# Strided attention on one core: full-width products on TensorE, a 32-bit turn of the weights, and one store with another wait

## The chip, the cores and the metric

The kernel runs on one core of a Trainium2 chip. The metric is the device time of one execution in microseconds (us). Before the change three runs took 128.56, 128.7 and 128.8 us; their median is 128.7 us. One further execution was recorded by the hardware profiler, and all rows of the profile come from it.

The core has five engines that run side by side and wait for each other by semaphores: TensorE (PE in the profile; PEld is its loading of weights), VectorE (DVE), ScalarE (ACT), GpSimd (POOL) and SyncE (SP). SP only issues transfers here. All transfers go through one queue.

## The reference, cut to what matters

```python
batch, heads, seq, dim = (8, 12, 1024, 64)     # stride = 64
for i in range(seq):
    attend_positions = np.arange(0, seq, stride)            # 16 keys for every query
    scores = np.einsum('bhqd,bhkd->bhqk', q, k) * scale     # scale = 1 / sqrt(dim)
    weights = np.exp(scores - np.max(scores, axis=-1, keepdims=True))
    weights = weights / (np.sum(weights, axis=-1, keepdims=True) + 1e-10)
    result[:, :, i, :] = np.einsum('bhqk,bhkd->bhqd', weights, v)[:, :, 0, :]
```

Every query of a head sees the same 16 keys (positions 0, 64, 128, ...). Q is read whole and the result is written whole, 25 MB each; of K and V only 16 rows a head are read.

## The kernel before, in words

**Groups.** The 96 heads are worked on in 24 groups of four heads. A group of Q is 1 MB: 128 partitions with 32 queries of 64 numbers each, so a partition holds 32 x 64 float32 values. A buffer of `big` (16 of them, `NB`) receives a group of Q and later takes the group's result, which is stored from there.

**The stages of a group g**, with the engine and the line that carries each in the profile:

1. SP loads Q into `big` (L34).
2. ACT casts one half of it to 16 bits into `qb` (L352), POOL the other half (L357).
3. DVE turns `qb` into `qt` (L361), with a transpose that works on blocks of 32 x 32 words; a word is a pair of 16-bit numbers (even and odd dimension of Q).
4. PE multiplies keys and `qt`, giving the scores in the PSUM bank `sc` (L557). A group has two pairs of heads (index b) and two halves of the queries (index e). For each half f of the dimension, each e and each b there is one product with 32 columns of weights, `k_cur`, which lands on its own 32 partitions of the bank: 8 products with 512 columns of `qt`.
5. DVE turns the scores into `s_t` (L392), so that a partition again holds its 32 queries with 16 scores each, and finds the maximum of each query (`top`, L399).
6. POOL subtracts it (`diff`, L406), ACT takes the exponential (`ex`, L412), DVE adds up (`total`, L417) and inverts (`rec`, L424), POOL multiplies (`w_n`, 16 bits, L431).
7. DVE turns the weights back (`w_t`, L437), as 128 x 512 numbers of 16 bits, in one instruction.
8. PE multiplies `w_t` and the values `v_cur` (L571): for each half h of the result four steps, each with two products of 64 x 64 weights, one on the partitions and outputs 0 to 63, one on 64 to 127: 16 products a group.
9. ACT evicts each half from PSUM into `big` (`evict`, L453), and SP stores it (L34).

**Keys and values.** All keys and values are loaded, cast and arranged at the start (lines 297 to 346). After that POOL copies the keys of the next two groups into `k_cur` (`place_k`) and the values of two groups into `v_cur` (`place_v`), both through the helper of L370.

**What sets the order.** The program is written out by hand in the loop of lines 503 to 546: step n deals with the scores of group n, the turn of Q of group n + 1, the sums of group n - 1, the turned weights and outputs of group n - 2, and so on. Each engine works through its own part of that list in order. VectorE's order in a round is: `s_t` of g, `qt` of g + 1, `top` of g, `total` of g - 1, `w_t` of g - 2, `rec` of g - 1. For groups 2 to 21 these rounds are a hardware loop (`dve_stream`); PE runs a loop over all groups (`pe_stream`), with the scores of group j + 3 ahead of the outputs of group j. So at the end it still computes scores for the groups 24 to 26, which do not exist; nobody reads them.

**Waits.** An instruction may count up a named "gate" (`ev` for evictions, `wt` for turned weights, `wn`, `ex`, `sc`, `turned`, `stK`, `stV`), or the general semaphore of its engine, not both. Whoever wants to wait for a gated instruction in the general way waits for the next ungated one of that engine instead (lines 103 to 110):

```python
while d is not None and self.ops[d]["gate"]:
    later = (j for j in range(d + 1, i) if self.ops[j]["lane"] == p["lane"])
    d = next(later, None)
```

The stores wait for evictions in this way. Before the change all evictions except those of the last group carry the gate `ev` (L454). So the store of the groups 20 and 21, which needs the eviction (21, 1), waits for the next ungated instruction of ACT after it, the eviction (23, 0). The last store, of the groups 22 and 23, is issued by itself after everything else (L631).

Of the kernel before, what the change touches and what calls it, by code (L numbers as in the profile page):

```python
# [174 lines left out]
def kernel(  # L175
# [8 lines left out]
    nc = tc.nc  # L184

    B, H, S, D = Q.shape
    NK = S // stride
# [27 lines left out]
    diff = [sb.tile([P, 32, NK], FP32, name=f"diff{i}") for i in range(2)]  # L215
# [58 lines left out]
    def constants():  # L274
        op("POOL", lambda: nc.gpsimd.memset(identity, 0.0), writes=["identity"])
        op("POOL", lambda: nc.gpsimd.affine_select(
            out=identity, in_=identity, compare_op=ALU.not_equal, fill=1.0, base=0,
            pattern=[[-1, P]], channel_multiplier=1,
        ), reads=["identity"], writes=["identity"])
        for c in range(2):  # L280
            for b in range(2):
                op("POOL", lambda c=c, b=b: nc.gpsimd.tensor_copy(
                    out=perm_v[:, c, b],
                    in_=_ap_with(
                        identity, [identity.ap[0], [0, 2], [32, 2], [1, NK]], 64 * c + 16 * b
                    ),
                ), reads=["identity"], writes=[f"perm{c}{b}"])
        op("DVE", lambda: nc.vector.memset(k_all, 0.0), writes=["k_zero"])
# [78 lines left out]
    def place(to, from_, g, n, needs, writes, gate):  # L367
        dims = "pgabx"[: len(to.shape)]
        flat = f"{' '.join(dims)} -> p ({' '.join(dims[1:])})"
        op("POOL", lambda: nc.gpsimd.tensor_copy(  # L370
            out=to[:, g % 2 : g % 2 + n].rearrange(flat).bitcast(I32),
            in_=from_[:, g : g + n].rearrange(flat).bitcast(I32),
        ), reads=needs, writes=writes, gate=None if g == 1 else gate)

    def place_k(g):
        n = 1 if g < 2 else 2
        place(k_cur, k_all, g, n,
              ["k_zero"] + [f"k{i % 2}{s}" for i in range(g, g + n) for s in range(4)],
              [f"k_cur{i % 2}" for i in range(g, g + n)], "stK")

    def place_v(g):
        n = 1 if g < 2 else 2
        place(v_cur, v_all, g, n,
              [f"v_all{i % 2}{x}" for i in range(g, g + n) for x in range(4)],
              [f"v_cur{i % 2}" for i in range(g, g + n)], "stV")

    def scores(g):
        op("PE", None, reads=[f"qt{g % 2}", f"k_cur{g % 2}"], writes=[f"sc{g % 2}"],
# [15 lines left out]

    def subtract(g):
        op("POOL", lambda: nc.gpsimd.tensor_tensor(  # L406
            out=diff[g % 2], in0=s_t[g % 2],
            in1=top[g % 2].unsqueeze(2).to_broadcast([P, 32, NK]), op=ALU.subtract,
        ), reads=[f"s_t{g % 2}", f"top{g % 2}"], writes=[f"diff{g % 2}"])

    def raise_(g):
        op("ACT", lambda: nc.scalar.activation(  # L412
            out=ex[g % 2][:, :, 0:NK], in_=diff[g % 2], func=AF.Exp, bias=0.0, scale=scale,
        ), reads=[f"diff{g % 2}"], writes=[f"ex{g % 2}"], gate="ex" if g < LAST - 1 else None)

    def sums(g):
        return nc.vector.tensor_reduce(out=total[g % 2], in_=ex[g % 2], op=ALU.add, axis=mybir.AxisListType.X)  # L417
# [11 lines left out]

    def normalise(g):  # L430
        op("POOL", lambda: nc.gpsimd.tensor_tensor(  # L431
            out=w_n[g % 2], in0=ex[g % 2][:, :, 0:NK],
            in1=rec[g % 2].unsqueeze(2).to_broadcast([P, 32, NK]), op=ALU.mult,
        ), reads=[f"ex{g % 2}", f"rec{g % 2}"], writes=[f"w_n{g % 2}"], gate="wn")

    def back(g):
        return nc.vector.transpose(  # L437
            _ap_with(w_t[g % 2], [w_t[g % 2].ap[0], [64, 8], [1, 2], [2, 32]]),
            w_n[g % 2].rearrange("p n k -> p (n k)"),
        )  # L440
# [9 lines left out]
    def evict(g, h):  # L450
        o = o_ps[h].rearrange("p c (t x d) -> p x (c t) d", t=2, d=D)
        to = big[:, g % NB].rearrange("p (x t d) -> p x t d", x=4, t=8)[:, :, 4 * h : 4 * h + 4]
        op("ACT", lambda: nc.scalar.copy(to, o), reads=[f"o{h}"], writes=[f"b{g % NB}{'ab'[h]}"],  # L453
           gate=None if g == NG - 1 else "ev")  # L454

    first_loads()
    constants()
# [35 lines left out]
    def on(f, g, *a, **how):  # L493
        if 0 <= g < NG:
            f(g, *a, **how)
# [7 lines left out]
    for n in range(NG + 4):  # L503
        how = dict(looped=FIRST <= n < LAST, late=n >= LAST)
        on(evict, n - 3, 1)
        if n < NG:
            spread(n, **how)
        if n == 0:
            maximum(n)
        on(turn_over, n + 1, **how)  # L510
        if n == 0:
            value_blocks(0, range(2, 4))
        elif n < NG:
            maximum(n, **how)
        on(add_up, n - 1, **how)
        on(weights_back, n - 2, **how)
        on(invert, n - 1, **how)
        if n == NG - 1:
            for g in range(AHEAD):
                op("DVE", lambda: nc.vector.nop(), gate="turned", late=True)  # L520
        if n % 2 and n > 1:
            next_keys(n + 1)
        on(cast_p, n + 2)
        if n % 2 == 0 and n > 2:
            on(place_v, n - 2)
        if n < NG:
            subtract(n)
        if n == 1:
            next_keys(n + 1)
        if n == 1 or n == 2:  # L530
            place_v(n - 1)
        on(normalise, n - 1)
        if n + 1 < NG + AHEAD:
            scores(n + 1)
        for h in range(2):
            on(outputs, n - 2, h)
        on(cast_a, n + 3)
        if n < NG:
            raise_(n)
        if n < 2:  # L540
            value_blocks(1, range(2 * n, 2 * n + 2))
        if n == 1:
            load(NB - 2)
            load(NB - 1)
        on(evict, n - 2, 0)
        issue(n - 3 if n + 3 < NG else n - 4)
    issue(NG, flush=True)

    def pe_stream(sems, gates):
        pe = nc.tensor  # L550

        def score_products(g):
            for f in range(2):
                for e in range(2):
                    for b in range(2):
                        c = 2 * b + e
                        r = pe.matmul(  # L557
                            sc_ps[g % 2][32 * c : 32 * c + 32], lhsT=k_cur[:, g % 2, f, b],
                            rhs=_ap_with(
                                qt[g % 2], [qt[g % 2].ap[0], [D, 8], [16 * D, 2], [2, 32]],  # L560
                                extra_offset=8 * D * e + f,
                            ),
                            start=f == 0, stop=f == 1, tile_position=(0, 32 * c),
                        )
            r.then_inc(gates["sc"], 1)

        def output_products(g, h):
            for t in range(4):
                for b in range(2):
                    half_b = slice(64 * b, 64 * b + 64)  # L570
                    r = pe.matmul(  # L571
                        o_ps[h][half_b, t // 2, 256 * (t % 2) : 256 * (t % 2) + 256],
                        lhsT=w_t[g % 2][half_b, 4 * h + t],
                        rhs=v_cur[half_b, g % 2].rearrange("p x d -> p (x d)"),
                        start=True, stop=True, tile_position=(64 * b, 64 * b),
                    )
            r.then_inc(sems["PE"], 1)

        pe.wait_ge(gates["stV"], 1)
# [86 lines left out]
```

## Time and profile before

| | |
|---|---|
| median of three runs | 128.7 us (128.56 to 128.8) |
| the profiled execution | 128.46 us, of which the profile's span is 126.6 us |
| busy: PE, DVE, ACT, POOL | 64.2, 100.5, 90.2, 84.2 us |
| moved | 51.15 MB, 404 GB/s over the span |
| read from and written to HBM | 25.95 and 25.17 MB |

The rows read as follows. A group's row gives line, engine, operation, the tile written and the tiles read, the shape, the count, then the busy time and the mean duration in ns of one, then the idle time of the engine ahead of them and what ended it. A timeline row gives start and length, then the instruction; "x8" means that eight were merged into one row. A row of a stretch (from:to) gives its length, busy time and count for PE, PEld, DVE, ACT and POOL, then the clock granted to TensorE as a share of full speed, the transfers' busy share, and GB/s. Durations can be longer than the distance to the next instruction, because an engine may begin the next one while the last one's end is still under way; the chain of waits shows the distance, a group's mean the duration.

### The profile page before, as it was taken

The page shows a single profiled execution, that of the slowest core. Times are in us where ns is not written, and L with a number is a line of the kernel's source. Part 1 is how long each engine was busy: PE and PEld are TensorE (multiplying, and loading weights), DVE is VectorE, ACT ScalarE, POOL GpSimd, SP SyncE. Part 2 cuts the span into 40 slices and gives each one's busy share as a digit, 9 for nine tenths or more (in the row PEclk, how much of TensorE's full clock was granted, in tenths as well). Part 3 has the DMA queues.
Part 4 walks back from the last instruction along what each step waited for, and adds up shares of the span by engine and source line. Part 5 has one row for each costly group of instructions (what it writes and reads, how often), then busy time and mean ns, then how long its engine had stood idle before and what let it go on. Part 6 is the DMA issues. An engine that isn't in the chain of part 4 may idle for free.

```text
span 126.6 us, 1871 instructions
## 1 busy us (share of the span) xinstructions
PE 64.2 (51%) x604; PEld 32.7 (26%) x604; DVE 100.5 (79%) x159; ACT 90.2 (71%) x106; POOL 84.2 (67%) x110
## 2 busy tenths in 40 slices
PE   0000702338777788777345777779755336970000
PEld 0000100004543245543112543335522213530000
DVE  4329699499999999999999999999999999520000
ACT  4016679557899988989999789998899669692000
POOL 4016742859888898888898888898888867600000
PEclk9999999999999999999999555555589998699555
DMA  3899999999999989999999989989899999988993
GB/s 93 311 405 441 404 466 445 393 445 404 476 435 393 445 362 422 479 399 396 479 386 430 500 352 453 479 349 494 378 430 430 425 430 425 425 347 342 414 414 166
DMA packets 6803, 51.15 MB, mean 404 GB/s; under 512 B 3760, under 2 KB 3760, under 8 KB 3760
## 3 DMA queue, kind: packets, MB, share of 16 engines
q1 hardware_dynamic: 6800, 51.12, 96.5%
q14 instruction: 3, 0.02, 0.1%
HBM read 25.95 MB, written 25.17 MB: 404 GB/s over the span
## 4 chain that ended last, share of the span: by engine, by line
DVE 68%; ACT 6%; DMA 5%; PE 5%; issue 3%; POOL 3%; DVEq 1%; SPq 0%
DVE qt L361 20%; DVE s_t L392 12%; DVE top L399 11%; DVE total L417 11%; DVE w_t L437 9%; DMA big<-in_K_dram 5%; DVE rec L424 3%; ACT big L453 3%; PE sc L557 2%; PE o L571 2%; DVE v_all L339 2%; POOL qb L357 1%; POOL diff L406 1%; ACT k_all L308 1%; ACT qb L352 1%
## 5 line engine op out<-in xcount | busy, mean ns | idle before, releaser
L453 ACT COPY big<-o 128x1024 f32<-128x1024 f32 x48 | 46.2, 1016 | 8.4 <-PE o L571 8.4
L571 PE MATMUL o<-v_cur,w_t 64*64 64x256 bf16 x384 | 38.5, 361 | 21.1 <-DVE w_t L437 18.6
L571 PEld LDWEIGHTS o<-v_cur,w_t 64*64 64x64 bf16 x384 | 28.7, 142 | 40.5 <-ACT big L453 27.2
L557 PE MATMUL sc<-qt,k_cur 128*32 128x512 bf16 x216 | 25.2, 557 | 15.4 <-DVE qt L361 10.0
L431 POOL TENSOR_TENSOR w_n<-ex,rec 128x512 bf16<-128x512 f32 x24 | 25.4, 1057 | 8.9 <-DVE rec L424 8.9
L406 POOL TENSOR_TENSOR diff<-s_t,top 128x512 f32<-128x512 f32 x24 | 25.4, 1058 | 7.9 <-DVE top L399 7.9
L361 DVE STREAM_TRANSPOSE qt<-qb 128x1024 int32<-128x1024 int32 x24 | 28.8, 1202 | 0.0
L352 ACT CAST qb<-big 128x1024 bf16<-128x1024 f32 x24 | 25.2, 1054 | 0.0
L357 POOL CAST qb<-big 128x1024 bf16<-128x1024 f32 x24 | 25.0, 1043 | 0.0
L412 ACT ACTIVATE ex<-diff 128x512 f32<-128x512 f32 x24 | 15.3, 638 | 6.2 <-POOL diff L406 6.1
L437 DVE STREAM_TRANSPOSE w_t<-w_n 128x512 bf16<-128x512 bf16 x24 | 17.9, 746 | 1.6 <-POOL w_n L431 1.5
L392 DVE STREAM_TRANSPOSE s_t<-sc 128x512 f32<-128x512 f32 x24 | 16.1, 671 | 1.6 <-PE sc L557 1.6
L417 DVE TENSOR_REDUCE total<-ex 128x32 f32<-128x544 f32 x24 | 17.0, 707 | 0.3 <-ACT ex L412 0.3
L399 DVE TENSOR_REDUCE top<-s_t 128x32 f32<-128x512 f32 x24 | 15.5, 647 | 0.1
L557 PEld LDWEIGHTS sc<-qt,k_cur 128*32 128x32 bf16 x216 | 3.6, 103 | 26.9 <-DVE qt L361 19.8
L315 PE MATMUL o<-big,perm_v 128*128 128x384 bf16 x4 | 1.5, 520 | 12.8 <-POOL big L323 12.8
L424 DVE RECIPROCAL rec<-total 128x32 f32<-128x32 f32 x24 | 7.4, 308 | 0.0
L370 POOL COPY v_cur<-v_all 128x256 int32<-128x256 int32 (+1 forms) x13 | 5.0, 384 | 1.1 <-PE o L571 1.1
L370 POOL COPY k_cur<-k_all 128x128 int32<-128x128 int32 (+1 forms) x13 | 3.7, 281 | 2.1 <-ACT k_all L308 1.8
L298 ACT CAST big<-big 128x384 bf16<-128x384 f32 x1 | 0.5, 511 | 5.6 <-DMA big<-in_K_dram 5.6
L299 POOL CAST big<-big 128x384 bf16<-128x384 f32 x1 | 0.5, 507 | 5.6 <-DMA big<-in_K_dram 5.6
L301 DVE STREAM_TRANSPOSE big<-big 128x384 int32<-128x384 int32 x1 | 0.6, 579 | 4.3 <-POOL big L299 4.3
(18 smaller groups left out, 18.8 us busy)
## 6 DMA issues: line engine op xcount, KB each, us to landing
big<-in_Q_dram SPq DMA_DIRECT2D x24, 1024.0 KB, 12.2
out_dram<-big SPq DMA_DIRECT2D x7, 2048.0 KB, 13.7
out_dram<-big SPq DMA_DIRECT2D x10, 1024.0 KB, 14.1
big<-in_K_dram SPq DMA_DIRECT2D x1, 384.0 KB, 6.8
big<-in_V_dram SPq DMA_DIRECT2D x1, 384.0 KB, 7.9
```

The source lines that it names most:

```text
L352: op("ACT", lambda: nc.scalar.copy(b[:, half:], q[:, half:]), reads=[f"b{g % NB}{h}" for h in "ab"], writes=[f"qb{g % 4}1"])
L357: op("POOL", lambda: nc.gpsimd.tensor_copy(out=b[:, 0:half], in_=q[:, 0:half]), reads=[f"b{g % NB}{h}" for h in "ab"] + [f"qb{g % 4}1"] * ...
L361: return nc.vector.transpose(qt[g % 2].bitcast(I32), qb[g % 4].bitcast(I32))
L392: return nc.vector.transpose(s_t[g % 2].rearrange("p n k -> p (n k)"), sc_ps[g % 2])
L399: return nc.vector.tensor_reduce(out=top[g % 2], in_=s_t[g % 2], op=ALU.max, axis=mybir.AxisListType.X)
L406: op("POOL", lambda: nc.gpsimd.tensor_tensor(out=diff[g % 2], in0=s_t[g % 2], in1=top[g % 2].unsqueeze(2).to_broadcast([P, 32, NK]), op=AL ...
L417: return nc.vector.tensor_reduce(out=total[g % 2], in_=ex[g % 2], op=ALU.add, axis=mybir.AxisListType.X)
L431: op("POOL", lambda: nc.gpsimd.tensor_tensor(out=w_n[g % 2], in0=ex[g % 2][:, :, 0:NK], in1=rec[g % 2].unsqueeze(2).to_broadcast([P, 32, N ...
L437: return nc.vector.transpose(_ap_with(w_t[g % 2], [w_t[g % 2].ap[0], [64, 8], [1, 2], [2, 32]]), w_n[g % 2].rearrange("p n k -> p (n k)"),)
L453: op("ACT", lambda: nc.scalar.copy(to, o), reads=[f"o{h}"], writes=[f"b{g % NB}{'ab'[h]}"], gate=None if g == NG - 1 else "ev")
L557: r = pe.matmul(sc_ps[g % 2][32 * c : 32 * c + 32], lhsT=k_cur[:, g % 2, f, b], rhs=_ap_with(qt[g % 2], [qt[g % 2].ap[0], [D, 8], [16 * D, ...
L571: r = pe.matmul(o_ps[h][half_b, t // 2, 256 * (t % 2) : 256 * (t % 2) + 256], lhsT=w_t[g % 2][half_b, 4 * h + t], rhs=v_cur[half_b, g % 2] ...
```

## The change

- **Scores.** `k_cur` becomes 128 x 2 x 2 x 160: the two blocks of 32 key columns stand at 32 and 96, with zeros at 0, 64 and 128. A product takes 128 columns of it, beginning at 32 or at 0, so that the keys meet the partitions of e = 0 or of e = 1 and zeros the others. Four products of full width are added up in the bank, in place of eight of 32 columns. `place_k` copies into the gaps' pattern.
- **Weights.** The normalised weights `w_n` are written so that a pair of queries lies in one 32-bit word: the output pattern has a step of two 16-bit numbers. `back` turns them as 32-bit words, in two instructions, one for the partitions 0 to 63 and one for 64 to 127, each into its own diagonal block of `w_t`, now 128 x 8 x 128 with zeros elsewhere.
- **Outputs.** Each step is one product of full width with that block matrix, 8 a group in place of 16.
- **Subtraction.** It writes into `s_t`, and `diff` goes away.
- **Start.** VectorE sets `k_cur` and both buffers of `w_t` to zero.
- **Store.** The eviction (21, 1) gives up its gate, so that the store of the groups 20 and 21 waits for it alone. An instruction of ACT that does nothing follows it and passes on the gate `ev`.

```diff
-    w_t = [sb.tile([P, 8, 64], BF16, name=f"w_t{i}") for i in range(2)]
+    w_t = [sb.tile([P, 8, P], BF16, name=f"w_t{i}") for i in range(2)]
...
-    k_cur = sb.tile([P, 2, 2, 2, 32], BF16, name="k_cur")
+    k_cur = sb.tile([P, 2, 2, 5 * 32], BF16, name="k_cur")
...
+        op("DVE", lambda: nc.vector.memset(k_cur, 0.0), writes=["k_cur0", "k_cur1"])
+        for i in range(2):
+            op("DVE", lambda i=i: nc.vector.memset(w_t[i], 0.0), writes=[f"w_t{i}"])
...
     def place_k(g):
         n = 1 if g < 2 else 2
+        gap = k_cur[:, 0, 0, 32:].bitcast(I32)
+        op("POOL", lambda: nc.gpsimd.tensor_copy(
+            out=_ap_with(gap, [gap.ap[0], [80, 2 * n], [32, 2], [1, 16]], 160 * (g % 2)),
+            in_=k_all[:, g : g + n].rearrange("p g f b x -> p (g f) b x").bitcast(I32),
...
     def subtract(g):
         op("POOL", lambda: nc.gpsimd.tensor_tensor(
-            out=diff[g % 2], in0=s_t[g % 2],
+            out=s_t[g % 2], in0=s_t[g % 2],
...
     def normalise(g):
         op("POOL", lambda: nc.gpsimd.tensor_tensor(
-            out=w_n[g % 2], in0=ex[g % 2][:, :, 0:NK],
-            in1=rec[g % 2].unsqueeze(2).to_broadcast([P, 32, NK]), op=ALU.mult,
+            out=_ap_with(w_n[g % 2], [w_n[g % 2].ap[0], [64, 8], [1, 2], [32, 2], [2, NK]]),
+            in0=ex[g % 2][:, :, 0:NK].rearrange("p (t x u) k -> p t x u k", x=2, u=2),
+            in1=rec[g % 2].rearrange("p (t x u) -> p t x u", x=2, u=2).unsqueeze(4).to_broadcast([P, 8, 2, 2, NK]),
+            op=ALU.mult,
...
     def back(g):
-        return nc.vector.transpose(
-            _ap_with(w_t[g % 2], [w_t[g % 2].ap[0], [64, 8], [1, 2], [2, 32]]),
-            w_n[g % 2].rearrange("p n k -> p (n k)"),
-        )
+        for b in range(2):
+            rows = slice(64 * b, 64 * b + 64)
+            r = nc.vector.transpose(
+                w_t[g % 2][rows, :, rows].bitcast(I32),
+                w_n[g % 2][rows].rearrange("p n k -> p (n k)").bitcast(I32),
+            )
+        return r
...
-           gate=None if g == NG - 1 else "ev")
+           gate=None if g == NG - 1 or (g, h) == (NG - 3, 1) else "ev")
...
         on(evict, n - 3, 1)
+        if n - 3 == NG - 3:
+            op("ACT", lambda: nc.scalar.nop(), reads=[f"b{(NG - 3) % NB}b"], gate="ev")
...
         def score_products(g):
+            for e in range(2):
+                for f in range(2):
+                    r = pe.matmul(
+                        sc_ps[g % 2], lhsT=k_cur[:, g % 2, f, 32 * (1 - e) : 32 * (1 - e) + P],
+                        rhs=_ap_with(
+                            qt[g % 2], [qt[g % 2].ap[0], [D, 8], [16 * D, 2], [2, 32]],
+                            extra_offset=8 * D * e + f,
+                        ),
+                        start=e + f == 0, stop=e + f == 2,
+                    )
...
         def output_products(g, h):
             for t in range(4):
+                r = pe.matmul(
+                    o_ps[h][:, t // 2, 256 * (t % 2) : 256 * (t % 2) + 256],
+                    lhsT=w_t[g % 2][:, 4 * h + t],
+                    rhs=v_cur[:, g % 2].rearrange("p x d -> p (x d)"),
+                    start=True, stop=True,
+                )
```

More of the change, by code (lines that the diff above doesn't have):

```diff
@@ L214 @@
     s_t = [sb.tile([P, 32, NK], FP32, name=f"s_t{i}") for i in range(2)]
-    diff = [sb.tile([P, 32, NK], FP32, name=f"diff{i}") for i in range(2)]
     ex = [sb.tile([P, 32, NK + 1], FP32, name=f"ex{i}") for i in range(2)]
     w_n = [sb.tile([P, 32, NK], BF16, name=f"w_n{i}") for i in range(2)]
-    w_t = [sb.tile([P, 8, 64], BF16, name=f"w_t{i}") for i in range(2)]
+    w_t = [sb.tile([P, 8, P], BF16, name=f"w_t{i}") for i in range(2)]
     top = [sb.tile([P, 32], FP32, name=f"top{i}") for i in range(2)]
@@ L365, in turn_over @@
            gate="turned", gates=[("qp", g + 1)], **how)
[L367 to L373, printed above, removed]
     def place_k(g):
         n = 1 if g < 2 else 2
-        place(k_cur, k_all, g, n,
-              ["k_zero"] + [f"k{i % 2}{s}" for i in range(g, g + n) for s in range(4)],
-              [f"k_cur{i % 2}" for i in range(g, g + n)], "stK")
+        gap = k_cur[:, 0, 0, 32:].bitcast(I32)
+        op("POOL", lambda: nc.gpsimd.tensor_copy(
+            out=_ap_with(gap, [gap.ap[0], [80, 2 * n], [32, 2], [1, 16]], 160 * (g % 2)),
+            in_=k_all[:, g : g + n].rearrange("p g f b x -> p (g f) b x").bitcast(I32),
+        ), reads=["k_zero"] + [f"k{i % 2}{s}" for i in range(g, g + n) for s in range(4)],
+           writes=[f"k_cur{i % 2}" for i in range(g, g + n)], gate=None if g == 1 else "stK")
     def place_v(g):
         n = 1 if g < 2 else 2
-        place(v_cur, v_all, g, n,
-              [f"v_all{i % 2}{x}" for i in range(g, g + n) for x in range(4)],
-              [f"v_cur{i % 2}" for i in range(g, g + n)], "stV")
+        op("POOL", lambda: nc.gpsimd.tensor_copy(
+            out=v_cur[:, g % 2 : g % 2 + n].rearrange("p g x d -> p (g x d)").bitcast(I32),
+            in_=v_all[:, g : g + n].rearrange("p g x d -> p (g x d)").bitcast(I32),
+        ), reads=[f"v_all{i % 2}{x}" for i in range(g, g + n) for x in range(4)],
+           writes=[f"v_cur{i % 2}" for i in range(g, g + n)], gate=None if g == 1 else "stV")
     def scores(g):
@@ L406, in subtract @@
         op("POOL", lambda: nc.gpsimd.tensor_tensor(
-            out=diff[g % 2], in0=s_t[g % 2],
+            out=s_t[g % 2], in0=s_t[g % 2],
             in1=top[g % 2].unsqueeze(2).to_broadcast([P, 32, NK]), op=ALU.subtract,
-        ), reads=[f"s_t{g % 2}", f"top{g % 2}"], writes=[f"diff{g % 2}"])
+        ), reads=[f"s_t{g % 2}", f"top{g % 2}"], writes=[f"s_t{g % 2}"])
     def raise_(g):
         op("ACT", lambda: nc.scalar.activation(
-            out=ex[g % 2][:, :, 0:NK], in_=diff[g % 2], func=AF.Exp, bias=0.0, scale=scale,
-        ), reads=[f"diff{g % 2}"], writes=[f"ex{g % 2}"], gate="ex" if g < LAST - 1 else None)
+            out=ex[g % 2][:, :, 0:NK], in_=s_t[g % 2], func=AF.Exp, bias=0.0, scale=scale,
+        ), reads=[f"s_t{g % 2}"], writes=[f"ex{g % 2}"], gate="ex" if g < LAST - 1 else None)
     def sums(g):
@@ L552, in score_products @@
         def score_products(g):
[L553 to L564, printed above, removed]
+            for e in range(2):
[8 more added lines that the diff above has]
+                    )
             r.then_inc(gates["sc"], 1)
@@ L568, in output_products @@
             for t in range(4):
[L569 to L576, printed above, removed]
+                r = pe.matmul(
[4 more added lines that the diff above has]
+                )
             r.then_inc(sems["PE"], 1)
```

## The prediction

> **What bounds the kernel now.** I read the page's chain of waits first, its shares by engine, then the chain in order of time, then the groups, the timeline of the start and of the end, and the transfers by stretches.
>
> ```profile
> DVE 68%; ACT 6%; DMA 5%; PE 5%; issue 3%; POOL 3%; DVEq 1%; SPq 0%
> ```
>
> VectorE is two thirds of the chain. One round of it, from the chain in order of time (start, length up to the next piece):
>
> ```profile
> 78.20 0.58 DVE s_t L392
> 78.78 1.12 DVE qt L361
> 79.90 0.57 DVE top L399
> 80.47 0.62 DVE total L417
> 81.09 0.66 DVE w_t L437
> 81.75 0.21 DVE rec L424
> ```
>
> Six instructions follow each other without a gap, 3.76 us a group, in some 20 looped rounds. VectorE sets the pace, but the end is a store's:
>
> ```profile
> 108.71 1.93 ACT L453 COPY big<-o 128x1024 f32<-128x1024 f32 x2 [1.02 <-PE o L571]
> 110.91 3.76 ACT L453 COPY big<-o 128x1024 f32<-128x1024 f32 x4 [0.27 <-PE o L571]
> ```
> ```profile
> 113.78 1.80 SPq L34 DMA_DIRECT2D out_dram<-big  x2
> ```
> ```profile
> 104.00:113.00 9.00, 7.04 (x82) 3.62 (x84) 5.81 (x11) 7.20 (x9) 4.82 (x6) 0.81 1.01 426
> 113.00:115.00 2.00, 0.51 (x8) 0.24 (x6) 0.00 (x0) 1.67 (x2) 0.00 (x0) 1.00 0.31 131
> 115.00:125.00 10.00, 0.00 (x0) 0.00 (x0) 0.00 (x0) 0.00 (x0) 0.00 (x0) 0.59 0.97 413
> 125.00:126.60 1.60, 0.00 (x0) 0.00 (x0) 0.00 (x0) 0.00 (x0) 0.00 (x0) 0.50 0.00 0
> ```
>
> The last two columns are the transfers' busy share and GB/s. Transfers are saturated until 113.4, then two thirds idle for 2 us (2 x 0.69 = 1.4 us lost), then busy for the 10 us of the last two stores, and 1.6 us close the span. The two lines of stores at the end are issued at 113.78 and about 115.0; bytes move again at about 115.0, so issue to first byte is 1.2 us. So two things stand close together at the end: when the last groups are evicted, and how much the queue still holds.
>
> **The store that waits less.** Before, the store of groups 20 and 21 waits for the third of the four evictions at 110.91 (110.91 + 3 x 0.94 = 113.73, issued at 113.78). After, it waits for group 21's own second eviction, which ends at 108.71 + 1.93 = 110.64. Alone this lets the first byte come at 111.84, ahead of 113.4, and removes the 1.4 us: a gain, if nothing else is late. The spare in it is 113.4 - 111.84 = 1.6 us. The NoOp that passes the gate on in ACT costs an estimated 0.1 us once, behind which evict(22, 1) stands; evict(22, 0) from 110.91 covers it (uncovered: 0.1 us).
>
> **The weights' turn, on the pace itself.** One 16-bit transpose of 128 x 512 becomes two 32-bit ones of 64 x 256 words, on partitions 0 to 63 and 64 to 127. Groups, and two stretches of VectorE's timeline:
>
> ```profile
> L361 DVE STREAM_TRANSPOSE qt<-qb 128x1024 int32<-128x1024 int32 x24 | 28.8, 1202 | 0.0
> L437 DVE STREAM_TRANSPOSE w_t<-w_n 128x512 bf16<-128x512 bf16 x24 | 17.9, 746 | 1.6 <-POOL w_n L431 1.5
> L392 DVE STREAM_TRANSPOSE s_t<-sc 128x512 f32<-128x512 f32 x24 | 16.1, 671 | 1.6 <-PE sc L557 1.6
> ...
> L308 DVE COPY k_all<-big 32x384 bf16<-32x384 bf16 x6 | 3.5, 577 | 0.1
> ```
> ```profile
> 8.81 0.58 DVE L301 STREAM_TRANSPOSE big<-big 128x384 int32<-128x384 int32 x1 [4.30 <-POOL big L299]
> 9.42 3.55 DVE L308 COPY k_all<-big 32x384 bf16<-32x384 bf16 x6
> ```
>
> Transposes of 32-bit words advance 1.12 us for 1024 and 0.58 for 512 elements, 1.055 ns an element, so 256 advance 0.58 - 0.27 = 0.31 us when the next instruction overlaps their end; their own duration is some 0.09 longer (671 ns against 580, 1202 against 1120), so 0.40. Low bound: two overlapped, 0.62 us against today's 0.66, a gain of 0.04 a round. High bound: the six copies of L308 start on other partitions than the one before (each output begins 32 partitions further or each input elsewhere), and they do not overlap at all: 6 x 0.577 = 3.46, in 3.55 us, 0.02 between them. Priced like this, the first transpose takes 0.40 + 0.02; the second starts alone, as L301's 384 words did, 0.58 - 128 x 0.001055 = 0.445, and 0.465 with the gap, since the reciprocal goes back to partition 0; the reciprocal, which starts alone too, I make 0.05 longer, as L392's turn is after a wait (0.72 at 25.14, quoted with the scores below, against 0.67 on average). Sum 0.42 + 0.465 + 0.05 = 0.935 against 0.66: some +0.27 us a round. I take 0.26, near the high bound, because L308's six are the only rows in which VectorE changes its starting partition. By the twenty-second turn, that of group 21, it is 22 x 0.26 = 5.7 us.
>
> The six copies are also shorter and narrower than everything around them, so the row alone could be read as a matter of size. The Trainium skill (VectorE: DVE Perf Modes, "Two Vector instructions with no wait between them") says that an instruction whose input or output starts in another group of 32 partitions than its predecessor's begins only when all earlier ones have finished. By that rule the second transpose and the reciprocal are both held, +0.27 a round; by size alone they overlap, -0.04. L308's 3.55 us agrees with the rule; no run here shows it for a transpose.
>
> **Scores on TensorE.** Eight products of 32 columns, four side by side, become four full-width ones in a row.
>
> ```profile
> 12.82 1.46 PE L315 MATMUL o<-big,perm_v 128*128 128x384 bf16 x4 [12.82 <-POOL big L323]
> ```
> ```profile
> 18.75 1.04 PE L557 MATMUL sc<-qt,k_cur 128*32 128x512 bf16 x8 [3.40 <-DVE qt L361]
> 20.13 0.70 DVE L392 STREAM_TRANSPOSE s_t<-sc 128x512 f32<-128x512 f32 x1
> 23.61 0.29 POOL L370 COPY k_cur<-k_all 128x128 int32<-128x128 int32 x1
> 24.05 1.04 PE L557 MATMUL sc<-qt,k_cur 128*32 128x512 bf16 x8 [4.25 <-POOL k_cur L370]
> 25.14 0.72 DVE L392 STREAM_TRANSPOSE s_t<-sc 128x512 f32<-128x512 f32 x1 [1.59 <-PE sc L557]
> ```
> ```profile
> 81.86 1.92 PE L571 MATMUL o<-v_cur,w_t 64*64 64x256 bf16 x16 [0.82 <-DVE w_t L437]
> 83.71 1.04 PE L557 MATMUL sc<-qt,k_cur 128*32 128x512 bf16 x8
> 85.65 0.72 DVE L392 STREAM_TRANSPOSE s_t<-sc 128x512 f32<-128x512 f32 x1
> ...
> 102.59 0.64 PE L557 MATMUL sc<-qt,k_cur 128*32 128x512 bf16 x8 [0.75 <-DVE qt L361]
> ```
> ```profile
> 70.00:93.00 23.00, 17.46 (x144) 9.55 (x144) 23.00 (x37) 20.35 (x25) 20.43 (x25) 0.50 1.01 430
> ```
>
> Four full-width products of 384 columns took 1.46 us, each with its own weights: 4 x 0.32 + 0.18, 0.83 ns a column. So 512 columns take 0.427, and four 4 x 0.427 + 0.18 = 1.89 us where eight took 1.04 (two steps of 0.427). That is the pace at granted clock 0.50 (the last row); the start has the same 1.04, and is priced by the durations. At full clock 0.64 becomes 0.64 + 2 x 0.213 = 1.07. In the loop, scores start at 83.71 and are read at 85.65, 1.94 later: 1.89 just fits, and a longer round gives more room. At the start nothing covers it. Group 1's scores end at 20.64, read at 20.70 instead of 20.13 (+0.57); through top, subtraction and keys this moves 24.05, and group 2's scores are waited for directly (+0.85). Sum +1.4 us, once. In the end the products for groups that don't exist (24 to 26) stand ahead of real outputs: 0 at full clock, +0.85 each at half; I take 0.5 in all.
>
> **Outputs on TensorE.** Eight pairs of 64 x 64 products become eight full-width ones: 8 x 0.213 + 0.2 = 1.9 us at half clock, today's 1.92. Nothing, since a pair ran side by side.
>
> **POOL.** The normalised weights go out every second 16-bit element, the keys with gaps.
>
> ```profile
> L406 POOL TENSOR_TENSOR diff<-s_t,top 128x512 f32<-128x512 f32 x24 | 25.4, 1058 | 7.9 <-DVE top L399 7.9
> L431 POOL TENSOR_TENSOR w_n<-ex,rec 128x512 bf16<-128x512 f32 x24 | 25.4, 1057 | 8.9 <-DVE rec L424 8.9
> ...
> L357 POOL CAST qb<-big 128x1024 bf16<-128x1024 f32 x24 | 25.0, 1043 | 0.0
> ...
> L370 POOL COPY v_cur<-v_all 128x256 int32<-128x256 int32 x11 | 4.4, 400 | 1.1 <-PE o L571 1.1
> ```
>
> 16-bit and 32-bit outputs cost the same (1057, 1058), so the output doesn't set the time; I take 0, bounds 0 and +1.06 (each output a step of its own). A round needs 1.06 + 1.06 + 1.04 + 0.35 (half of v_cur's 0.40 and of k_cur's 0.29 at 23.61) = 3.51 of 3.76, of the new round of 4.02 still less: up to 0.5 us would be hidden, the rest paid each round. The subtraction in place needs no new wait: the next write of that buffer follows on VectorE the row sum, which has waited for the exponential.
>
> **Three memsets** of zeros go on VectorE.
>
> ```profile
> L288 DVE MEMSET k_all<- 128x1536 uint32 x1 | 1.3, 1338 | 1.9 <-issue 1.9
> ```
>
> They are 2 x 512 and 320 words, so by k_all's 1536 in 1.34 us some 1.3 us with their own starts. L301 has 4.30 us of idle time before it, until the keys arrive: covered (uncovered +1.3).
>
> **Sum.** Group 21's second eviction moves by 1.4 + 5.7 + 0.5 = 7.6 to 118.2; first byte 119.4; two stores 10.0; close 1.6: 131.0. The last store: its eviction (110.91 + 3.76 = 114.67) moves by 7.6 and another 0.3 for group 22's turn, to 122.6, first byte 1.5 later at 124.1, 5.0 for its half, 1.6: 130.7. So 131.0, +4.4 on 126.6, and the profiled time 128.46 becomes 132.9. The median of the three runs shown, 128.7, lies 0.24 above that execution: 133.1.
>
> **Rivals.** *Half the price* (+0.13 a round, one of the two starts overlaps): 1.4 + 2.9 + 0.5 = 4.8; the same sum gives 128.2, time 130.3.
> *No hold at all, faster*: the transposes overlap like all other neighbours in a round. 1.4 - 0.9 + 0.5 = 1.0 is under the 1.6 spare, and the transfers run through: 113.4 + 10.0 + 1.6 = 125.0, time 127.1. For it: every row with 128 partitions overlaps. Against: L308. It decides below a shift of 126.6 - 1.6 - 10.0 - 1.2 - 110.64 = 3.2 us, that is below 0.06 a round.
> *POOL takes the pace*: w_n doubles to 2.1, a round needs 4.57, 0.8 more than 3.76; 22 x 0.8 + 1.9 = 19.5 of shift, time about 145. Against: the equal 1057 and 1058.
> *The scores aren't waited for at the start* (full clock there): the 1.4 falls away, 131.7; the pace decides all the same. Against: 1.04 in both rows.
>
> **Numbers.** Forecast 0.62 (own range 131.8 to 135, the price between 0.20 and 0.34), half price 0.13, no hold 0.15, POOL 0.06, a stall that I don't see 0.04. The range 128.6 to 135.2 leaves out no hold and POOL. A measurement tells some 0.2% from no change: faster 0.15, within 0.05 (between half price and none), slower 0.80.
>
> **What would show it.** The two transposes 0.4 to 0.45 us each without overlap and a round of 4.02 in the chain; scores 1.89 at the start and s_t of group 2 at 26.5 (25.14 + 1.4); w_n still 1.06; the store issued right after its eviction, at 118, with transfers idle before it. A round of 3.75 or less would make the forecast wrong.

## The result, and the profile after

The changed kernel takes 132.08 us (median of six runs, 131.96 to 132.23), the kernel before 128.59 us in the runs beside it: a ratio of 1.0269, with a 95% interval of 1.0256 to 1.0283. It is slower, inside the forecast's range (128.6 to 135.2), 1.0 us below the predicted 133.1. The profiled execution took 132.23 us, its span is 130.4 us.

First the groups that answer to the quoted ones, from the page of the changed kernel:

```profile
L430 POOL TENSOR_TENSOR w_n<-ex,rec 128x512 bf16<-128x512 f32 x24 | 25.5, 1063 | 16.5 <-DVE rec L423 16.5
...
L440 DVE STREAM_TRANSPOSE w_t<-w_n 64x256 int32<-64x256 int32 x48 | 20.9, 435 | 1.8 <-POOL w_n L430 1.5
...
L423 DVE RECIPROCAL rec<-total 128x32 f32<-128x32 f32 x24 | 8.5, 353 | 0.7
```

The weights' turn costs 48 x 435 ns = 20.9 us of VectorE instead of 17.9, the reciprocal 353 ns instead of 308. POOL's product is unmoved (1063 against 1057). One round of the chain of waits, then the same turns in VectorE's timeline, then the distance of four rounds:

```profile
78.45 0.34 DVE w_t L440
78.81 0.44 DVE w_t L440
79.28 0.35 DVE rec L423
79.64 0.57 DVE s_t L391
80.20 1.12 DVE qt L363
81.33 0.57 DVE top L398
81.89 0.63 DVE total L416
82.52 0.34 DVE w_t L440
```
```profile
78.37 0.88 DVE L440 STREAM_TRANSPOSE w_t<-w_n 64x256 int32<-64x256 int32 x2
79.28 0.35 DVE L423 RECIPROCAL rec<-total 128x32 f32<-128x32 f32 x1
79.55 0.65 DVE L391 STREAM_TRANSPOSE s_t<-sc 128x512 f32<-128x512 f32 x1
```
```profile
43.60 1.12 DVE qt L363
...
59.87 1.12 DVE qt L363
```

A piece of the chain begins where the one ahead of it ends, so an instruction that overlaps the one ahead is shown too short there; the timeline has its true start. The turns start at 78.37 and 78.81, the reciprocal at 79.28, `s_t` at 79.55: 0.44, 0.47 and 0.27 us, together 1.18. The first two distances are as long as the turns or longer (435 ns on average, 0.88 us for both together), so neither the second turn nor the reciprocal begins before all ahead of it has ended. `s_t` does, 0.08 us before the reciprocal's end.

A round is 82.52 - 78.45 = 4.07 us, and so is the mean of four (16.27 / 4). Before, most rounds took 3.76, every fourth was longer, and the mean of four was 15.14 / 4 = 3.78; here are the two rows of before that give it:

```profile
41.00 1.13 DVE qt L361
...
56.14 1.12 DVE qt L361
```

The start, from the timeline of VectorE of the changed kernel:

```profile
26.61 0.72 DVE L391 STREAM_TRANSPOSE s_t<-sc 128x512 f32<-128x512 f32 x1 [2.40 <-PE sc L561]
```

Group 2's scores are turned at 26.61 instead of 25.14. And the end, from ACT's timeline, SP's timeline and the stretches:

```profile
115.75 1.93 ACT L457 COPY big<-o 128x1024 f32<-128x1024 f32 x2 [0.37 <-PE o L573]
```
```profile
117.71 0.54 SPq L34 DMA_DIRECT2D out_dram<-big  x1
```
```profile
110.00:113.00 3.00, 2.44 (x10) 1.02 (x9) 2.92 (x7) 1.12 (x3) 1.81 (x2) 0.56 0.00 0
113.00:118.00 5.00, 4.33 (x26) 2.11 (x25) 4.17 (x9) 4.32 (x5) 2.97 (x5) 0.92 0.98 419
118.00:119.00 1.00, 1.00 (x9) 0.56 (x6) 0.10 (x1) 0.93 (x2) 0.87 (x1) 1.00 0.50 213
119.00:129.00 10.00, 1.40 (x10) 0.71 (x8) 0.78 (x2) 2.92 (x4) 0.00 (x0) 0.75 0.94 398
```

Group 21's second eviction ends at 115.75 + 1.93 = 117.68, 7.04 us later than before, and its store is issued at once, at 117.71. The transfers now wait for the groups: nothing moves from 110 to 113, little at 118 to 119. Then the last two stores take their 10 us.

### The profile page after: what moved, and what is told of

Read it like the earlier page. It is cut to its first block, busy times and chain, and to the rows that moved or that the text cites. A ratio compares the mean times of both kernels' runs of the same rounds, so it can differ in the third digit from the quotient of the medians.

```text
span 130.4 us, 1299 instructions
## 1 busy us (share of the span) xinstructions
PE 69.8 (54%) x304; PEld 29.6 (23%) x304; DVE 108.0 (83%) x186; ACT 91.0 (70%) x106; POOL 84.2 (65%) x110
## 4 chain that ended last, share of the span: by engine, by line
DVE 68%; DMA 6%; PE 6%; issue 5%; POOL 4%; SPq 2%; DVEq 1%; ACT 1%; ACTq 1%; POOLq 0%
DVE qt L363 20%; DVE w_t L440 11%; DVE top L398 11%; DVE total L416 11%; DVE s_t L391 10%; DMA big<-in_V_dram 6%; DVE rec L423 6%; PE sc L561 4%; POOL w_n L430 2%; SPq L34 1%; PE o L317 1%; POOL s_t L405 1%; ACT big L457 1%; ACTq L161 1%; POOL big L325 1%
## 5 line engine op out<-in xcount | busy, mean ns | idle before, releaser
L561 PE MATMUL sc<-qt,k_cur 128*128 128x512 bf16 x108 | 37.5, 480 | 23.0 <-DVE qt L363 18.4
L573 PE MATMUL o<-v_cur,w_t 128*128 128x256 bf16 x192 | 31.2, 317 | 15.4 <-DVE w_t L440 13.7
L430 POOL TENSOR_TENSOR w_n<-ex,rec 128x512 bf16<-128x512 f32 x24 | 25.5, 1063 | 16.5 <-DVE rec L423 16.5
L405 POOL TENSOR_TENSOR s_t<-s_t,top 128x512 f32<-128x512 f32 x24 | 25.4, 1059 | 9.2 <-DVE top L398 9.2
L573 PEld LDWEIGHTS o<-v_cur,w_t 128*128 128x128 bf16 x192 | 19.7, 110 | 34.1 <-issue 27.9
L411 ACT ACTIVATE ex<-s_t 128x512 f32<-128x512 f32 x24 | 15.2, 634 | 10.5 <-POOL s_t L405 10.5
L440 DVE STREAM_TRANSPOSE w_t<-w_n 64x256 int32<-64x256 int32 x48 | 20.9, 435 | 1.8 <-POOL w_n L430 1.5
L561 PEld LDWEIGHTS sc<-qt,k_cur 128*128 128x128 bf16 x108 | 9.5, 108 | 43.8 <-DVE qt L363 27.8
L423 DVE RECIPROCAL rec<-total 128x32 f32<-128x32 f32 x24 | 8.5, 353 | 0.7
L310 DVE COPY k_all<-big 32x384 bf16<-32x384 bf16 x6 | 3.5, 590 | 0.1
```

The source lines that it names most:

```text
L405: op("POOL", lambda: nc.gpsimd.tensor_tensor(out=s_t[g % 2], in0=s_t[g % 2], in1=top[g % 2].unsqueeze(2).to_broadcast([P, 32, NK]), op=ALU ...
L430: op("POOL", lambda: nc.gpsimd.tensor_tensor(out=_ap_with(w_n[g % 2], [w_n[g % 2].ap[0], [64, 8], [1, 2], [32, 2], [2, NK]]), in0=ex[g % 2 ...
L440: r = nc.vector.transpose(w_t[g % 2][rows, :, rows].bitcast(I32), w_n[g % 2][rows].rearrange("p n k -> p (n k)").bitcast(I32),)
L561: r = pe.matmul(sc_ps[g % 2], lhsT=k_cur[:, g % 2, f, 32 * (1 - e) : 32 * (1 - e) + P], rhs=_ap_with(qt[g % 2], [qt[g % 2].ap[0], [D, 8], ...
L573: r = pe.matmul(o_ps[h][:, t // 2, 256 * (t % 2) : 256 * (t % 2) + 256], lhsT=w_t[g % 2][:, 4 * h + t], rhs=v_cur[:, g % 2].rearrange("p x ...
```

## The experiments

Each kernel was timed beside the kernel before, whose median was 128.65 us in each comparison. The theory had three parts: the second turn and its neighbours pay for starting on other partitions; the wider scores cost only at the start; the earlier store removes 1.4 us of idle transfers. The first two stood, the third fell.

### The store alone

```diff
-           gate=None if g == NG - 1 else "ev")
+           gate=None if g == NG - 1 or (g, h) == (NG - 3, 1) else "ev")
...
+        if n - 3 == NG - 3:
+            op("ACT", lambda: nc.scalar.nop(), reads=[f"b{(NG - 3) % NB}b"], gate="ev")
```

> The kernel before with the earlier store alone (the eviction (21, 1) gives up its gate, the instruction that does nothing follows it). My theory, that the transfers are the bound at the end and stood 1.4 us idle at 113 to 115: they run through, 127.0 us (about -1.6 us), evictions unmoved at 110.64 and 114.67, the last byte at about 123.4. Rival, that the last store decides alone because it is issued last at 115.0: no change, 128.6 us.

Measured: 128.67 us, ratio 1.000 (0.9987 to 1.0013). No gain. The stretches of this run:

```profile
113.00:115.00 2.00, 0.34 (x8) 0.07 (x2) 0.00 (x0) 1.50 (x2) 0.00 (x0) 1.00 0.97 410
115.00:123.00 8.00, 0.00 (x0) 0.00 (x0) 0.00 (x0) 0.00 (x0) 0.00 (x0) 0.60 1.01 430
123.00:125.00 2.00, 0.00 (x0) 0.00 (x0) 0.00 (x0) 0.00 (x0) 0.00 (x0) 0.50 0.12 49
```

The hole at 113 to 115 is filled (0.97 instead of 0.31), and a new one stands at 123 to 125 (0.12; the kernel before has 0.81 there). The busy share is a mean over 16 transfer engines, and it hid that one of them was late. The trace has 16 small completion writes for each transfer, one from each engine; these are the times of the first, the fifteenth and the last of the 16, worked out from the trace's transfer records:

```
store of groups    18 and 19                20 and 21                22 and 23
before             113.00 114.08 115.22     119.92 120.05 120.13     124.79 124.91 125.05
store alone        113.22 114.00 115.46     118.13 118.91 120.37     123.03 123.82 125.28
one turn           113.03 113.97 114.94     117.94 118.88 119.85     122.85 123.79 124.76
same partition     113.17 114.63 114.66     118.08 119.56 119.57     122.99 124.48 124.50
turn and store     113.14 114.16 115.36     118.05 119.07 120.27     122.96 123.97 125.19
wide, old wait     113.09 113.87 114.83     120.91 121.03 121.04     125.77 125.89 125.91
wide, new wait     113.05 114.11 115.09     117.96 119.02 120.01     122.87 123.93 124.93
old wait, changed  117.37 117.50 117.53     126.85 126.97 126.99     131.71 131.84 131.85
changed            118.26 118.39 118.40     123.81 123.94 123.95     128.76 128.89 128.89
```

In the kernel before, fifteen engines were done with the store of groups 18 and 19 at 114.08 and waited for the next one, whose bytes came at about 115.0. The last was done at 115.22: it never waited. Feeding the fifteen sooner lets them finish sooner, at 123.82, and the last one ends at 125.28, no sooner than before (125.05). The trace doesn't name the engines; that the last one is the same in each store is read from its even steps (115.46, 120.37, 125.28, 4.91 us each).

### The scores narrow again

```diff
-            for e in range(2):
-                for f in range(2):
+            for f in range(2):
+                for e in range(2):
+                    for b in range(2):
...
-                        sc_ps[g % 2], lhsT=k_cur[:, g % 2, f, 32 * (1 - e) : 32 * (1 - e) + P],
+                        sc_ps[g % 2][32 * c : 32 * c + 32], lhsT=k_cur[:, g % 2, f, 64 * b + 32 : 64 * b + 64],
```

> The changed kernel with the scores as eight products of 32 columns again (on the keys with gaps); all else as changed. My theory, that full-width scores cost only at the start (s_t of group 2 at 26.6 instead of 25.1) and are covered in the loop: s_t of group 2 back at 25.2, the round unchanged at 4.07 us, time 130.6 us (132.1 - 1.5). Rival, that TensorE's longer scores also lengthen the loop's round: the round falls below 4.0 us and the time below 129.5 us.

Measured: 130.9 us, ratio 1.0175 (1.0158 to 1.0192), 1.2 us less than the changed kernel. From its VectorE timeline and its chain of waits:

```profile
24.89 0.72 DVE L391 STREAM_TRANSPOSE s_t<-sc 128x512 f32<-128x512 f32 x1 [1.59 <-PE sc L563]
```
```profile
62.22 1.12 DVE qt L363
...
66.28 1.12 DVE qt L363
```

The start is back at 24.89, and the round is unmoved, 4.06 us. So the width of the scores is no part of the round. The start gives back 26.61 - 24.89 = 1.72 us, but the time only 1.2. The rest goes at the end: the outputs of group 21 take longer here than in the changed kernel (1.03, quoted further down), at a lower clock of TensorE:

```profile
113.46 1.46 PE L575 MATMUL o<-v_cur,w_t 128*128 128x256 bf16 x8
```

Its evictions begin at 114.51, 1.05 us behind the start of these products, against 0.63 in the changed kernel.

### One turn in place of two

```diff
-        for b in range(2):
-            rows = slice(64 * b, 64 * b + 64)
-            r = nc.vector.transpose(
-                w_t[g % 2][rows, :, rows].bitcast(I32),
-                w_n[g % 2][rows].rearrange("p n k -> p (n k)").bitcast(I32),
-            )
-        return r
+        return nc.vector.transpose(
+            w_t[g % 2].rearrange("p t m -> p (t m)").bitcast(I32),
+            w_n[g % 2].rearrange("p n k -> p (n k)").bitcast(I32),
+        )
```

`w_t` is 64 wide again here, with the 16 output products of before.

> The changed kernel with one 32-bit turn of 128 x 256 words, into weights of 64 columns, and the 16 output products of 64 x 64 of before; full-width scores and earlier store as changed. My theory, that the second turn and the two starts on other partitions are the price: the turn advances 0.31 us, the round falls from 4.07 to about 3.5 us, where POOL's 3.51 us take the pace, and the end is held by the transfers alone, 127.0 us. Rival, that a 32-bit turn or the normalised weights' pattern is itself costly: the round stays above 3.78 us and the time above 128.6 us. Second rival, that full-width scores at half clock (1.7 us for them and 1.7 us for the outputs) take the pace: a round of 3.6 to 3.8 us, and a time between 127.0 and 128.

Measured: 128.25 us, ratio 0.9982 (0.9968 to 0.9996). From its chain:

```profile
65.28 0.35 DVE w_t L438
65.64 0.24 DVE rec L423
65.87 0.57 DVE s_t L391
```

The turn and the reciprocal take 0.59 us, half of the changed kernel's 1.18. A 32-bit turn is cheap, then, also against the 16-bit one (0.66). Most rounds take 3.47 us and one in four is longer, 3.57 on average, near the 3.5 of the theory and below what either rival said. The time falls only to 128.25, not to 127.0: the transfers hold it (the table).

### Two turns from the same partition

```diff
-                w_t[g % 2][rows, :, rows].bitcast(I32),
-                w_n[g % 2][rows].rearrange("p n k -> p (n k)").bitcast(I32),
+                (w_t[g % 2][0:64, :, 0:64], w_x[g % 2][0:64])[b].bitcast(I32),
+                w_n[g % 2][0:64].rearrange("p n k -> p (n k)").bitcast(I32),
```

> The changed kernel, but the second turn of each group also works on the partitions 0 to 63, into a tile that nobody reads; the weights of the partitions 64 to 127 are left out, so half of the result is zero. Two turns of 64 x 256 words as in the changed kernel; only the starting partition of the second differs. My theory, that the price lies in the change of the starting partition: the two advance 0.31 us each and the reciprocal 0.21 to 0.23 us, the round falls from 4.07 to about 3.75 us, and the time to 127.0 to 127.5 us, where the transfers hold it. Rival, that two instructions of this size cost this much wherever they start: round 4.07 us, time 132.1 us.

Measured: 127.94 us, ratio 0.9949 (0.9933 to 0.9966), a little above the forecast time. From VectorE's timeline:

```profile
67.16 0.43 DVE L440 STREAM_TRANSPOSE w_t<-w_n 64x256 int32<-64x256 int32 x1
67.52 0.40 DVE L440 STREAM_TRANSPOSE w_x<-w_n 64x256 int32<-64x256 int32 x1
67.84 0.30 DVE L424 RECIPROCAL rec<-total 128x32 f32<-128x32 f32 x1
68.08 0.64 DVE L392 STREAM_TRANSPOSE s_t<-sc 128x512 f32<-128x512 f32 x1
```

Here the second turn and the reciprocal each begin 0.07 to 0.08 us before the one ahead has ended. Two instructions of 64 x 256 words and the reciprocal take 0.92 us together instead of 1.18, and the round is 3.80. This decides between the theory and the rival of size: 0.26 us of a round come from the starting partition. A second instruction costs something by itself, 0.92 against the 0.59 of the single turn. The second turn's output also differs here, as `w_x` is 64 wide and has no gaps; the next run shows that this doesn't matter.

### The outputs narrow again

The changed kernel with `w_t` 64 wide and 16 products, and its two turns as they are.

```diff
-                w_t[g % 2][rows, :, rows].bitcast(I32),
+                w_t[g % 2][rows].rearrange("p t m -> p (t m)").bitcast(I32),
```

> The changed kernel with the 16 output products of 64 x 64 of before, and weights of 64 columns that the same two turns of 64 x 256 words fill; scores, turns and store as changed. My theory, that the width of the outputs costs nothing while VectorE sets the pace: round 4.07 us and 132.1 us, as the changed kernel. Rival, that the full-width outputs have a share in the loss: below 131.5 us.

Measured: 132.05 us, ratio 1.0287 (1.0239 to 1.0335): the changed kernel's time. The round is 4.07 us, and the page has 435 ns for a turn and 353 for the reciprocal, the changed kernel's values. The width of the outputs costs nothing. Both turns write a tile without gaps here, so the shape of the output isn't the price of the turns either.

### One turn and the earlier store, all else as before

```diff
-            _ap_with(w_t[g % 2], [w_t[g % 2].ap[0], [64, 8], [1, 2], [2, 32]]),
-            w_n[g % 2].rearrange("p n k -> p (n k)"),
+            w_t[g % 2].rearrange("p t m -> p (t m)").bitcast(I32),
+            w_n[g % 2].rearrange("p n k -> p (n k)").bitcast(I32),
```

The pattern of `normalise` is the changed kernel's, and the store's edit is the one shown above.

> The kernel before with one 32-bit turn of 128 x 256 words and the earlier store; narrow scores and 64 x 64 outputs as before. VectorE's round is 3.45 us, so that groups are evicted 6 us earlier. My theory after the first four runs, that from a pace of 3.8 us down the slowest of the 16 transfer engines holds the end: 128.2 to 128.7 us, no change that matters. Rival, that the earlier evictions let the transfers start and end earlier: 127 us or less.

Measured: 128.54 us, ratio 0.9989 (0.998 to 0.9999). From ACT's timeline, the last six evictions:

```profile
103.63 5.81 ACT L455 COPY big<-o 128x1024 f32<-128x1024 f32 x6 [0.33 <-PE o L575]
```

VectorE's round is 3.57 on average (3.47 for most), as with one turn in the changed kernel. All groups are out at 109.44, five microseconds earlier than before, and the last completion stands at 125.19 in the table above. The work of the engines is not the bound from there on.

### The wide scores alone, with the old wait and with the new

```diff
-            for f in range(2):
-                for e in range(2):
-                    for b in range(2):
-                        c = 2 * b + e
+            for e in range(2):
+                for f in range(2):
...
-                        start=f == 0, stop=f == 1, tile_position=(0, 32 * c),
+                        start=e + f == 0, stop=e + f == 2,
```

> The kernel before with the full-width scores alone (with their keys and one memset), the old wait of the store. My theory: s_t of group 2 at 26.6 instead of 25.1, the round still 3.78 us; the store of groups 20 and 21 is issued 1.5 us later, at 115.3, and its bytes come at 116.5, when the slowest transfer engine has been free since 115.2: 1.3 us longer, 129.9 us. Rival, that the transfers cover the start: 128.6 us. Second rival, that at half clock the longer scores also reach into the round: above 130.5 us.

> The full-width scores with the earlier store, all else as before. My theory, that the earlier store has no worth of its own but is spare for a late eviction: the store is issued at about 112.0, its bytes come at 113.2, ahead of the slowest engine's 115.2, and the time is 128.6 us again, 1.3 less than with the old wait. Rival, that the store's wait doesn't matter: the same 129.9 us as with the old wait.

Measured: 129.28 us with the old wait, ratio 1.006 (1.0036 to 1.0083), and 128.37 us with the new one, 0.998 (0.997 to 0.9989). The runs of the first spread from 128.67 to 130.11, more than those of any other kernel here; why is open. Its store is issued at 114.77, so that its bytes come at about 116.0, when the last transfer engine has been done since 114.83 (the table):

```profile
114.77 1.80 SPq L34 DMA_DIRECT2D out_dram<-big  x2
```

The last completion is at 125.91, 0.9 us later than before. With the new wait the store's bytes are there in time, the last completion is at 124.93, and the late start costs nothing. So the earlier store has a worth only where the evictions are late.

### The changed kernel with the old wait

```diff
-           gate=None if g == NG - 1 or (g, h) == (NG - 3, 1) else "ev")
+           gate=None if g == NG - 1 else "ev")
...
-        if n - 3 == NG - 3:
-            op("ACT", lambda: nc.scalar.nop(), reads=[f"b{(NG - 3) % NB}b"], gate="ev")
```

> The changed kernel with the old wait of the store (for the eviction (23, 0)), all else as changed. My theory: the store is issued when that eviction ends, at about 121.6 instead of 117.7, and with the transfers idle until then the end moves by as much: 3.9 us, 136.0 us. Rival, that the store's wait doesn't matter, as in the run of it alone: 132.1 us.

Measured: 135.6 us, ratio 1.0561 (1.0527 to 1.0594), 3.5 us above the changed kernel. Its stretches:

```profile
118.00:122.00 4.00, 1.92 (x12) 0.90 (x10) 0.88 (x2) 3.08 (x4) 0.00 (x0) 1.00 0.10 41
122.00:132.00 10.00, 0.00 (x0) 0.00 (x0) 0.00 (x0) 0.00 (x0) 0.00 (x0) 0.64 0.95 403
```

Here all 16 engines wait (117.5 to 122 in the table and the stretch), and so the wait is paid.

## Why the prediction was right, and where it was not

**The weights' turn: right, by its mechanism.** Forecast: 0.42 and 0.465 for the two turns, 0.05 on the reciprocal, +0.26 a round. Measured: 0.44 and 0.47 for the turns and 0.045 on the reciprocal (353 against 308 ns); the usual round went from 3.76 to 4.07 (+0.31), the mean from 3.78 to 4.07 (+0.28). The run with two turns from the same partition shows that the starting partition is the cause, and the copies of L308 were the right row to price it by. The Trainium skill's rule (VectorE: DVE Perf Modes, "Two Vector instructions with no wait between them") holds for the transposes too: the reciprocal, which starts on partition 0 behind a turn on 64, begins at 79.28 in the changed kernel, after the turns' end at 79.25, and in that run at 67.84, before the turn's end at 67.92.

**The scores at the start: right.** +1.4 forecast, 26.61 - 25.14 = 1.47 measured; undone, the start is back and the round stays.

**The end on TensorE: wrong in sign, small.** The forecast added 0.5 us for products that nobody reads, at half clock. The turns and the start make 22 x 0.28 + 1.47 = 7.6 us, and group 21's eviction moved by 7.04: the end gave back 0.6. There TensorE ran at the pace of full clock, from these rows of the changed kernel's timeline:

```profile
114.21 1.07 PE L561 MATMUL sc<-qt,k_cur 128*128 128x512 bf16 x4 [0.46 <-DVEq L526]
115.12 1.03 PE L573 MATMUL o<-v_cur,w_t 128*128 128x256 bf16 x8
```

The kernel before had 1.91 us for the same outputs:

```profile
107.61 1.91 PE L571 MATMUL o<-v_cur,w_t 64*64 64x256 bf16 x16
```

The scores ahead of them, which nobody reads, took 1.07 us and not the 1.89 of half clock. The evictions of the group began 0.63 us behind the start of its outputs (115.75 - 115.12), against 1.10 before (108.71 - 107.61): 0.47 of the 0.6. That the clock was full at this place was luck: in the run with narrow scores the same outputs took 1.46. So 1.1 us lie between the forecast's 0.5 and the 0.6 given back; the round's 0.02 more over 22 rounds takes back 0.4. The span came out at 130.4 against 131.0, and the rest of the 1.0 us is that the changed kernel's runs lie 0.15 us below their profiled execution, where those of before lay 0.24 above.

**The store: the step that failed.** "Alone this lets the first byte come at 111.84, ahead of 113.4, and removes the 1.4 us: a gain, if nothing else is late." Alone it removes nothing. The forecast read a mean over 16 engines as if it were one queue; the slowest had no hole to fill, being done at 115.22 when the next bytes came at about 115.0. The sum was right all the same, because it went by another way: issue, 1.2 us, 10.0 us for two stores, close. Where all engines wait, as in the changed kernel, that is what happens (117.71 + 1.2 + 10.0 = 128.9; last completion 128.89).

**The rivals.** With the price of the turn gone, the time was to be 127.1. It is 127.9 to 128.7 in the five runs without that price in which the store is early, and 128.65 before: the floor of the transfers, not 127.1. So with the transfers as they are the kernel could not have become more than some 0.5% faster, and the 15% for that case rested on a gain that was not there. POOL's pace was rightly doubted: 1063 against 1057 ns.

**What stays open.** Which transfer engine is the last, and what it loses its 1.0 to 1.5 us on, was not tried. In the kernel before it isn't lost at once: the last completion lies 0.24, 0.43, 0.61, 0.85 and 1.14 us behind the fifteenth in the five stores that end from 94.7 to 115.2. The run with two turns from the same partition is 0.3 us below the best of the others, and its last engine is level with the fifteenth (124.50 and 124.48); half of its result is zero, and whether that has to do with it is open.

The best runs with a whole result, 128.25 and 128.37 us, lie 0.2% below the kernel before, with intervals that end just under 1 (0.9996 and 0.9989); that is too little to call them faster.

## What to carry to other kernels

Splitting one VectorE instruction by partitions costs more than two instructions: where the second half starts on another partition, it and the next instruction each lose the overlap with the one before, here 0.26 us of a 4.07 us round that VectorE sets. A hole in the transfers' busy share is a gain only if all engines wait in it; compare the last completion of a transfer with the moment at which the next one's bytes come. And a wait that costs nothing today (the store's) is spare: as soon as the work behind it is late, it is worth all of its length, 3.5 us here.

## What the runs showed of the hardware

The wider scores kept TensorE's clock up, which the forecast had not considered. The clock's row of the page, first of the kernel before, then of the one with the wide scores and the earlier store alone:

```profile
PEclk9999999999999999999999555555589998699555
```
```profile
PEclk9999999999999999999999999999999999999555
```

The stretch from 40 to 110 us, of before and then of that run:

```profile
40.00:110.00 70.00, 46.74 (x456) 25.42 (x456) 69.03 (x112) 61.26 (x73) 59.89 (x72) 0.80 1.00 426
```
```profile
40.00:110.00 70.00, 40.01 (x380) 21.20 (x379) 69.51 (x113) 62.54 (x73) 60.76 (x73) 1.00 1.00 424
```

The mean granted clock is 1.00 with the wide scores and 0.80 without, at VectorE's same round. The first slices of the clock's rows say full in both, but the scores took 1.04 and 1.89 us there, the lengths of half clock; in the kernel before they did so up to 57.32, so its 0.80 is still too high. The other kernels go the same way: over the whole span 0.89 to 0.97 in the 20 runs of the wide scores alone, 0.75 to 0.85 in those of the kernel before; at the round of 4.07, 0.835 to 0.88 in the changed kernel and 0.72 to 0.81 with its scores narrow.

TensorE's lower busy time (40.01 us against 46.74) doesn't speak against a clock that follows how busy TensorE is, because products at full clock are shorter. At one and the same speed the wide scores keep it busy for longer. These are rows at full clock, of before and of that run:

```profile
104.48 1.06 PE L571 MATMUL o<-v_cur,w_t 64*64 64x256 bf16 x16 [1.25 <-issue]
```
```profile
62.25 1.07 PE L555 MATMUL sc<-qt,k_cur 128*128 128x512 bf16 x4 [0.80 <-DVE qt L362]
64.19 1.06 PE L569 MATMUL o<-v_cur,w_t 64*64 64x256 bf16 x16 [0.86 <-DVE w_t L435]
```

With the narrow scores' 0.64 (at 102.59) a round of before has 1.70 us of products, a round with wide scores 2.13. The Trainium skill (TensorE: Matmul & The Clock Gate, "Part 1: The HAM clock gate") lets the clock follow how busy TensorE has been; these rows agree. Whether the share of the array that a product fills also counts was not tried by itself. For the outputs it made no difference: 0.835 to 0.881 with pairs of 64 x 64, 0.835 to 0.88 with full width, in two kernels that are otherwise equal.
